# Pre-norming the next tile's input through a ring in unused FFN scratch, loading the residual copy afterwards, and new transfer constants for the scheduler

## The chip, the cores and the metric

One Trainium2 chip, all 8 cores of it (cores 0 to 3 are one die, 4 to 7 the other). Each core runs the same program on its own half of a sequence. The metric is the device time of the slowest core in microseconds. In the profiles PE is TensorE (matmuls), DVE VectorE, ACT ScalarE, POOL GpSimd and SP SyncE; L482 is line 482 of the kernel, and a bracket at the end of a line gives the idle time before it and what ended it.

A program on all 8 cores has two states here. In a *fast* execution the cores end close together (0.2 to 0.8% apart in most). In a *slow* one the cores of one die, sometimes of both, show a lower granted TensorE clock and end later, by 1.5 to 18% here. The value of a die is the median of its four spans; it counts as undisturbed if that lies within 0.3% of the lowest die of the same kernel's runs.

## The reference, cut to what matters

Four layers. Even ones mix tokens by a gated unit (mixer A), odd ones by causal pooling (mixer B). Each is followed by a SwiGLU FFN, and each half-layer has a norm before and after:

```python
for i in range(DEPTH):                        # DEPTH = 4
    h = rmsnorm(x, mix_pre_g[i])              # pre-norm
    m = mixer_a(h, ...) if i % 2 == 0 else mixer_b(h, ...)
    x = x + rmsnorm(m, mix_post_g[i])         # post-norm, residual
    h = rmsnorm(x, ffn_pre_g[i])
    f = swiglu(h, ...)
    x = x + rmsnorm(f, ffn_post_g[i])
```

x is (4, 8192, 1024) in float32. A core takes 4096 tokens and a halo of 256, in five tiles: a short first one (384 + 384 tokens) and four of 512 + 384. All four layers run on a tile before the next tile is loaded.

## The kernel before

The author writes tasks, a list scheduler simulates them with costs of its own, and the order it finds is what each engine executes. On the chip an engine goes through its list in order (in the changed kernel VectorE stood 6.11 us at one multiply whose load was late, and SQF, the next of its list, behind it); only the semaphore waits adjust to what really happens. The scheduler's picture of transfers is one server:

```python
    DMA_BW = 230e3          # bytes per us
    DMA_LAT = 2.2           # us
    # ... in place():
            if t.dma is not None:
                server[0] = max(server[0], now + 0.5) + t.dma / self.DMA_BW
                t.finish = server[0] + self.DMA_LAT
```

A pre-norm is: eight Squares on ScalarE into SQ, their running sum on VectorE (ACC, then SQF), one matmul with a matrix of ones that sums over partitions, Ln and Exp for 1/rms (RS), and eight multiplies on VectorE that write H, the operand of the next matmuls. After the last FFN of a tile the chain of a half (`v.h` is 0 for the 512 tokens, 1 for the 384) is:

```python
        def add(fc):
            # ... o is MS when this is the tile's last layer, X otherwise
            # o = MS * g + X                      (VectorE, line L605)
            if final is not None:
                y0, nx = final
                t_dma("sp", (0, s, v.h, fc), yT3[:, fc, y0:y0 + v.n], m, ...)   # store
                if nx is not None:
                    load_x(nx[0], v.h, nx[1], fc, s)       # next tile, into X, in place
            if st is not None:
                st.add(fm(X, nxt[0], fc), ...)             # Square and sum of the new X
        # ... mult and add for all eight fc, then
        if st is not None:
            st.rstd()
            prenorm_apply(nxt[0], s, nxt[1])               # H of the next tile
```

So the next tile's X can be loaded only when the last residual add has read the old one. Weights go through six slots of 1 MB (WR), filled by loads that GpSimd's queue issues and that convert float32 to bf16 on the way (1024 KB each in the trace); X, stores and constants are issued by SyncE's queue. BIG is a scratch of 32 chunks per half; an FFN uses 22 of them.

## Time and profile before

| | us |
|---|---|
| timed runs | 6520.97, 6594.38 (slow), 6279.75, later 6280.7 (fast) |
| profiled run (fast), eight cores | 6258.5 to 6284.9, granted clock 0.967 to 0.970 |
| PE idle in gaps over 0.15 us | 429 to 459, by core |
| PE idle between two tiles, core 3 | 29.5 at the first change, 38 to 40 at the other three |

The views that carry the argument are shown in the prediction. One more belongs here, because it says how the 40 us at a tile change come about: the DMA queues between 2323 and 2372 us, core 3 of the kernel before. The first two lines are packets, MB and the share of the 16 engines' time, the others the loads, KB each and median us from issue to landing.

```profile
q0 software_dynamic: 864, 6.29, 80.8%
q1 hardware_dynamic: 1336, 2.45, 16.2%
...
WR<-wa_in POOLq DMA_DIRECT2D x6, 1024.0 KB, 16.0
...
X<-xT SPq DMA_DIRECT2D x8, 256.0 KB, 32.7
```

Six weight loads that nobody needs yet (PE has no H to multiply them with) take five times as much of the DMA engines as the X loads and stores that everything waits for. A load of a quarter of the size lands after twice the time.

That the weights are what delays X at a tile change is read from this view and from the X loads' times; no run held the weights back there (run 8 does so at the program's start alone).

### The profile page before, as it was taken

How to read it: one execution, taken by the hardware profiler on the slowest of the kernel's cores; microseconds unless marked ns; L12 is line 12 of the kernel's file. 1: busy time of each engine (PE TensorE's matmuls, PEld its weight loads, DVE VectorE, ACT ScalarE, POOL GpSimd, SP SyncE). 2: the span in 40 equal slices, each digit the busy share in tenths (PEclk: the TensorE clock that was granted, in tenths of full speed). 3: DMA queues.
4: the chain of work that ended last, by engine and by line, in shares of the span. 5: the costliest groups of instructions: out<-in, count | busy, mean ns of one | idle time of the engine just before them, and what ended most of it. 6: DMA issues, size and time to landing. Idle time of an engine off the chain costs nothing.

```text
span 6284.9 us, 92435 instructions; the slowest of 8 cores (6258.5 to 6284.9 us)
## 1 busy us (share of the span) xinstructions
PE 5807.5 (92%) x33076; PEld 3088.8 (49%) x33076; DVE 2703.9 (43%) x4972; ACT 2505.9 (40%) x5135; POOL 257.3 (4%) x489
## 2 busy tenths in 40 slices
PE   5989887999999997999999969999999789999998
PEld 2655554444545543455544534554455345554554
DVE  3443533436353624443545245353634252635262
ACT  4343442525252515342534244245324342525252
POOL 0000000000000000000000000000000000000000
PEclk9999988999999998999999989999999899999999
DMA  6667778443554454444544445444444444454443
GB/s 134 116 108 115 132 132 151 79 85 75 96 96 78 79 98 101 87 87 82 96 88 84 78 91 101 98 82 88 82 95 81 107 89 74 85 97 81 74 89 76
DMA packets 117567, 592.36 MB, mean 94 GB/s; under 512 B 28032, under 2 KB 40704, under 8 KB 50944
## 3 DMA queue, kind: packets, MB, share of 16 engines
q0 software_dynamic: 69840, 507.82, 45.7%
q1 hardware_dynamic: 47280, 78.63, 3.8%
q8 instruction: 274, 4.49, 0.3%
q14 instruction: 173, 1.42, 0.1%
HBM read 1070.60 MB, written 23.59 MB: 174 GB/s over the span
## 4 chain that ended last, share of the span: by engine, by line
PE 77%; DVE 10%; issue 5%; DMA 4%; ACT 3%; SPq 0%; DVEq 0%; ACTq 0%
PE ps L482 77%; DVE ACC L546 3%; DMA X<-xT 3%; DVE MS L599 3%; DVE H L574 1%; ACT RS L463 1%; ACT SQ L463 1%; DVE MS L765 1%; DVE X L605 1%; ACT BIG L463 1%; DVE SQF L549 1%; DMA w_s<-BIG 1%; ACT L463 1%; SPq L492 0%; DVE BIG L735 0%
## 5 line engine op out<-in xcount | busy, mean ns | idle before, releaser
L482 PE MATMUL ps<-H,WR 128*128 128x384 bf16 (+3 forms) x16640 | 2980.7, 342 | 58.4 <-DVE H L574 45.3
L482 PEld LDWEIGHTS ps<-H,WR 128*128 128x128 bf16 x16640 | 1599.9, 98 | 1418.4 <-issue 104.5
L482 PE MATMUL ps<-BIG,WR 128*128 128x384 bf16 (+4 forms) x10880 | 1955.1, 340 | 14.8 <-ACT SQ L463 4.7
L482 PEld LDWEIGHTS ps<-BIG,WR 128*128 128x128 bf16 x10880 | 1041.5, 98 | 904.8 <-issue 45.7
L662 DVE TENSOR_TENSOR BIG<-ps,SG 128x384 bf16<-128x384 f32 (+5 forms) x880 | 515.7, 590 | 1554.7 <-PE ps L482 1424.6
L463 ACT ACTIVATE SG<-ps 128x384 bf16<-128x384 f32 (+5 forms) x880 | 448.7, 517 | 1597.4 <-PE ps L482 1590.9
L546 DVE TENSOR_TENSOR ACC<-ACC,SQ 128x384 f32<-128x384 f32 (+5 forms) x960 | 566.9, 593 | 857.9 <-ACT SQ L463 785.0
L482 PE MATMUL ps<-WR,H 128*128 128x512 bf16 x3216 | 736.0, 390 | 40.0 <-DVE H L574 38.1
L463 ACT ACTIVATE MS<-ps 128x384 f32<-128x384 f32 (+5 forms) x640 | 332.5, 520 | 1035.1 <-PE ps L482 1033.5
L463 ACT ACTIVATE BIG<-ps 128x512 bf16<-128x512 f32 (+2 forms) x914 | 479.7, 564 | 325.0 <-PE ps L482 282.3
L482 PEld LDWEIGHTS ps<-WR,H 128*128 128x128 bf16 x3216 | 319.3, 100 | 439.6 <-issue 89.0
L463 ACT ACTIVATE SQ<-X 128x384 bf16<-128x384 f32 (+4 forms) x640 | 343.2, 556 | 317.1 <-DMA X<-xT 136.2
L599 DVE TENSOR_TENSOR MS<-MS,RS 128x384 f32<-128x384 f32 (+5 forms) x640 | 367.6, 585 | 211.5 <-ACT RS L463 211.5
L463 ACT ACT_TABLE_LOAD x257 | 329.7, 1283 | 238.6 <-PE ps L482 205.3
L574 DVE SCALAR_TENSOR_TENSOR H<-X,GV,RS 128x384 bf16<-128x384 f32 (+4 forms) x640 | 371.1, 650 | 102.3 <-ACT RS L463 102.1
L605 DVE SCALAR_TENSOR_TENSOR X<-MS,GV,X 128x384 f32<-128x384 f32 (+5 forms) x560 | 356.0, 646 | 0.1
L463 ACT ACTIVATE SQ<-ps 128x384 bf16<-128x384 f32 (+5 forms) x640 | 329.5, 522 | 21.2 <-DVE ACC L546 12.6
L482 PE MATMUL ps<-SQF,ONESM 128*128 128x384 bf16 (+5 forms) x160 | 57.6, 360 | 279.0 <-DVE SQF L549 278.0
L765 DVE SCALAR_TENSOR_TENSOR MS<-ps,GV,BIAS 128x384 f32<-128x384 f32 (+2 forms) x320 | 197.1, 656 | 107.9 <-PE ps L482 107.7
L492 POOL DMA_DIRECT2D WR<-wf_gu x220 | 116.1, 528 | 2641.8 <-PE ps L482 2625.6
L544 DVE CAST ACC<-SQ 128x384 f32<-128x384 bf16 (+4 forms) x160 | 57.7, 372 | 309.6 <-ACT SQ L463 309.4
L463 ACT ACTIVATE RS<-ps,EPSC 128x384 f32<-128x384 f32 (+5 forms) x160 | 98.0, 613 | 215.4 <-PE ps L482 214.4
(45 smaller groups left out, 1234.6 us busy)
## 6 DMA issues: line engine op xcount, KB each, us to landing
WR<-wf_gu POOLq DMA_DIRECT2D x220, 1024.0 KB, 10.1
WR<-wf_dn POOLq DMA_DIRECT2D x120, 1024.0 KB, 8.6
WR<-wa_in POOLq DMA_DIRECT2D x80, 1024.0 KB, 11.3
WR<-wa_out POOLq DMA_DIRECT2D x40, 1024.0 KB, 10.5
WR<-wb_in POOLq DMA_DIRECT2D x20, 1024.0 KB, 10.2
WR<-w_s SPq DMA_DIRECT2D x20, 1024.0 KB, 7.4
X<-xT SPq DMA_DIRECT2D x48, 192.0 KB, 7.2
BIAS<-bias_s SPq DMA_DIRECT2D x9, 1024.0 KB, 7.9
```

The lines of the kernel that those rows point to most:

```text
L463: return e.activation(out=out() if callable(out) else out, in_=in_() if callable(in_) else in_, func=func, **kw)
L482: return e.matmul(out(), lhsT=lhsT() if callable(lhsT) else lhsT, rhs=rhs() if callable(rhs) else rhs, start=start, stop=stop)
L492: return e.dma_start(out=out() if callable(out) else out, in_=in_)
L544: t_dve(self.prio + (1,), lambda e: e.tensor_copy(out=acc, in_=o()), [kq], [ka], v.n, 2)
L546: t_dve(self.prio + (1,), lambda e: e.tensor_tensor(out=acc, in0=acc, in1=o(), op=ALU.add), [kq, ka], [ka], v.n)
L549: t_dve(self.prio + (1,), lambda e: e.tensor_tensor(out=fin, in0=acc, in1=o(), op=ALU.add), [kq, ka], [kfin], v.n)
L574: t_dve(CH + (s, v.h, 1), lambda e, o=o, a=a, g=g, r=r: e.scalar_tensor_tensor(out=o, in0=a, scalar=g, in1=r, op0=ALU.mult, op1=ALU.mult), ...
L599: t_dve(CH + (s, v.h, 0), lambda e: e.tensor_tensor(out=m, in0=m, in1=r, op=ALU.mult), kf("MS", v, fc) + [("RS", v.h)], kf("MS", v, fc), v.n)
L605: t_dve(CH + (s, v.h, 0), lambda e: e.scalar_tensor_tensor(out=o, in0=m, scalar=g, in1=x, op0=ALU.mult, op1=ALU.add), kf("MS", v, fc) + kf ...
L662: t_dve((0, s, v.h), lambda e, o=o, sg=sg, bu=bu: e.tensor_tensor(out=o, in0=bank(bu, 0, v.n), in1=sg(), op=ALU.mult), [bu, ksg], ko, v.n)
L765: t_dve((0, s, v.h), lambda e, b=b, o3=o3, bb=bb, lg=lg: e.scalar_tensor_tensor(out=o3, in0=bank(b, 0, nl * 128).rearrange("p (c t) -> p c ...
```

## The change

Intent: while the last FFN of a tile runs, chunks 22 to 31 of BIG are free. Stream the next tile's x through three float32 slots there, twice. The first pass makes the sum of squares and 1/rms, the second, as soon as the FFN head (its gate and up projections) no longer reads H, writes the next tile's H. X itself is loaded after the final add as before, but is now needed only by the residual add behind the next mixer. The scheduler's transfer constants are changed too, to two servers.

```diff
-    DMA_BW = 230e3
-    DMA_LAT = 2.2
+    DMA_BW = {"pool": 320e3, "sp": 150e3}
+    DMA_LAT = {"pool": 3.5, "sp": 5.0}
@@ place()
-                server[0] = max(server[0], now + 0.5) + t.dma / self.DMA_BW
-                t.finish = server[0] + self.DMA_LAT
+                server[e] = max(server[e], now + 0.5) + t.dma / self.DMA_BW[e]
+                t.finish = server[e] + self.DMA_LAT[e]
@@ class Stats: accumulator, final sum and result may lie in the ring; Squares keep their order (cut)
+    def prefetch(s, tok0, v, gcol):
+        h, n, hw = v.h, v.n, HW[v.h]
+        base = 22 * hw
+        # f32(lo, w): a float32 view of BIG from base + lo (cut)
+        def load(fc):
+            o, ko = f32((fc % 3) * 2 * hw, n)
+            t_dma("sp", (1, s, h, fc), o, xT3[:, fc, tok0:tok0 + n], [], ko, 128 * n * 4, psem[h][fc % 3])
+            return o, ko
+        st = Stats(v, (2, s, h), acc=..., fin=...)
+        held = {}
+        for fc in range(KC):
+            held[fc] = o, ko = load(fc)
+            st.add(o, ko, False)
+        st.rstd()
+        for i in range(KC):
+            fc = (i + KC - 3) % KC
+            a, ka = held[fc] if i < 3 else load(fc)
+            # H[fc] = a * g[fc] * r      (VectorE, line L621)
@@ chain()
-        st = Stats(nxt[0], CH + (s, v.h)) if nxt is not None else None
+        st = Stats(nxt[0], CH + (s, v.h)) if nxt is not None and final is None else None
-            if st is not None:
+            elif st is not None:
@@ the last FFN of a tile, between head and down projection
+            if s % 8 == 7 and t + 1 < NTILES:
+                for h in range(2):
+                    prefetch(s, tile_geo(t + 1)[h][0], nxt[h][0], nxt[h][1])
```

More of the change, by code (lines that the diff above doesn't have):

```diff
@@ L132, in place @@
         aset = [None]
-        server = [0.0]
+        server = {"pool": 0.0, "sp": 0.0}
         order = []
@@ L528, in build_nc, with __init__ @@
     class Stats:
-        def __init__(self, v, prio):
-            self.v, self.prio, self.i = v, prio, 0
+        def __init__(self, v, prio, acc=None, fin=None):
+            self.v, self.prio, self.i, self.last = v, prio, 0, None
+            self.acc, self.ka = acc or (ACC[v.h][:, v.c0:v.c1], [("ACC", v.h)])
+            self.fin, self.kfin = fin or (SQF[v.h][:, v.c0:v.c1], [("SQF", v.h)])
+            self.r, self.kr = acc or (RS[v.h][:, v.c0:v.c1], [("RS", v.h)])
         def add(self, src, ksrc, psum, aset=None):
@@ L536, in add @@
             kq, o = tmp(SQ, "SQ", v.n)
-            t_act(self.prio + (0,), o, src, AF.Square, ksrc, [kq], v.n, psum, alloc=kq)
+            t = t_act(self.prio + (0,), o, src, AF.Square, ksrc, [kq], v.n, psum, alloc=kq)
+            if self.last is not None:
+                t.preds.setdefault(self.last, -1.0)
+            self.last = t
             i = self.i
             self.i += 1
-            acc = ACC[v.h][:, v.c0:v.c1]
-            fin = SQF[v.h][:, v.c0:v.c1]
-            ka, kfin = ("ACC", v.h), ("SQF", v.h)
+            acc, fin, ka, kfin = self.acc, self.fin, self.ka, self.kfin
             if i == 0:
-                t_dve(self.prio + (1,), lambda e: e.tensor_copy(out=acc, in_=o()), [kq], [ka], v.n, 2)
+                t_dve(self.prio + (1,), lambda e: e.tensor_copy(out=acc, in_=o()), [kq], ka, v.n, 2)
             elif i < KC - 1:
                 t_dve(self.prio + (1,), lambda e: e.tensor_tensor(out=acc, in0=acc, in1=o(), op=ALU.add),
-                      [kq, ka], [ka], v.n)
+                      [kq] + ka, ka, v.n)
             else:
                 t_dve(self.prio + (1,), lambda e: e.tensor_tensor(out=fin, in0=acc, in1=o(), op=ALU.add),
-                      [kq, ka], [kfin], v.n)
+                      [kq] + ka, kfin, v.n)
         def rstd(self):
@@ L554, in rstd @@
             b = Var("pss")
-            fin = SQF[v.h][:, v.c0:v.c1]
-            r = RS[v.h][:, v.c0:v.c1]
+            fin, r, kr = self.fin, self.r, self.kr
             t_pe((-1,) + self.prio, [(lambda: bank(b, 0, v.n), ONESM[:], fin, True, True,
-                                      [("SQF", v.h), ("ONESM",)], [b], v.n)], alloc=b)
-            t_act(self.prio + (0,), r, lambda: bank(b, 0, v.n), AF.Ln, [b, ("EPSC",)], [("RS", v.h)], v.n,
+                                      self.kfin + [("ONESM",)], [b], v.n)], alloc=b)
+            t_act(self.prio + (0,), r, lambda: bank(b, 0, v.n), AF.Ln, [b, ("EPSC",)], kr, v.n,
                   bias=EPSC[:], aset="ln")
-            t_act(self.prio + (0,), r, r, AF.Exp, [("RS", v.h)], [("RS", v.h)], v.n, False, scale=-0.5, aset="ln")
+            t_act(self.prio + (0,), r, r, AF.Exp, kr, kr, v.n, False, scale=-0.5, aset="ln")
     CH = (1,)
@@ L590, in build_nc, with f32 @@
     yT3 = yT.rearrange("(fc p) t -> p fc t", p=128)
+    psem = [[newsem() for _ in range(3)] for _ in range(2)]
+    def prefetch(s, tok0, v, gcol):
+        h, n, hw = v.h, v.n, HW[v.h]
+        base = 22 * hw
+        def f32(lo, w):
+            return BIG[h][:, base + lo:base + lo + 2 * w].bitcast(F32), blocks(h, base + lo, 2 * w)
+        def load(fc):
+            o, ko = f32((fc % 3) * 2 * hw, n)
+            t_dma("sp", (1, s, h, fc), o, xT3[:, fc, tok0:tok0 + n], [], ko, 128 * n * 4, psem[h][fc % 3])
+            return o, ko
+        st = Stats(v, (2, s, h), acc=f32(6 * hw, n), fin=(BIG[h][:, base + 8 * hw:base + 8 * hw + n],
+                                                           blocks(h, base + 8 * hw, n)))
+        held = {}
[6 more added lines that the diff above has]
+            a, ka = held[fc] if i < 3 else load(fc)
+            o, g = fm(H, v, fc), GV[:, gcol + fc: gcol + fc + 1]
+            t_dve((2, s, h), lambda e, o=o, a=a, g=g: e.scalar_tensor_tensor(
+                out=o, in0=a, scalar=g, in1=st.r, op0=ALU.mult, op1=ALU.mult),
+                ka + st.kr + [("GV",)], kf("H", v, fc), n)
     def chain(v, s, gpost, nxt, final=None):
         r = RS[v.h][:, v.c0:v.c1]
-        st = Stats(nxt[0], CH + (s, v.h)) if nxt is not None else None
+        st = Stats(nxt[0], CH + (s, v.h)) if nxt is not None and final is None else None
         def mult(fc):
```

## The prediction

> **What bounds the kernel now.** I began with the spans of the eight cores (6258 to 6285 us, clock 0.967 to 0.970: the profiled execution is a fast one, although two of the three timed runs, 6520.97 and 6594.38 us, are not), then the page's busy line.
>
> ```profile
> PE 5807.5 (92%) x33076; PEld 3088.8 (49%) x33076; DVE 2703.9 (43%) x4972; ACT 2505.9 (40%) x5135; POOL 257.3 (4%) x489
> ```
>
> TensorE is the bound; what can be won is its idle time, 6284.9 - 5807.5 = 477 us, plus matmuls that run on a reduced clock. Next I took the list of waits (total, times, longest), to see who keeps PE and ScalarE idle.
>
> ```profile
> DVE ACC L546 <- ACT SQ L463: 785.0, 340, 13.9
> PE ps L482 <- DVE SQF L549: 278.0, 54, 49.1
> ACT SQ L463 <- DMA X<-xT: 136.2, 38, 13.9
> PE ps L482 <- DVE H L574: 83.4, 33, 6.0
> ```
>
> PE's largest wait is for the sum of squares (SQF) of a norm. SQF waits for Squares, Squares for the input load. To see where, I read PE's timeline at the change from the second tile to the third (start, duration, then in brackets the idle time before and its releaser).
>
> ```profile
> 2321.40 24.86 PE L482 MATMUL ps<-BIG,WR 128*128 128x384 bf16 x152
> 2364.03 0.48 PE L482 MATMUL ps<-SQF,ONESM 128*128 128x384 bf16 x1 [17.76 <-DVE SQF L549]
> 2383.13 0.58 PE L482 MATMUL ps<-SQF,ONESM 128*128 128x512 bf16 x1 [18.62 <-DVE SQF L549]
> 2386.33 29.51 PE L482 MATMUL ps<-WR,H 128*128 128x512 bf16 x128 [2.62 <-DVE H L574]
> ...
> 2445.65 0.48 PE L482 MATMUL ps<-SQF,ONESM 128*128 128x384 bf16 x1 [5.15 <-DVE SQF L549]
> 2449.57 23.41 PE L482 MATMUL ps<-WR,H 128*128 128x512 bf16 x96 [3.44 <-DVE H L574]
> ```
>
> The last down projection ends at 2346.26, and the new tile's first matmul starts at 2386.33: 17.76 + 18.62 + 2.62 = 39.0 us idle. The second token half follows only at 2449.57, after another 8.6 us in the last two lines. ScalarE's timeline there says why:
>
> ```profile
> 2345.84 0.63 ACT L463 ACTIVATE SQ<-X 128x512 bf16<-128x512 f32 x1 [8.42 <-DMA X<-xT]
> 2360.24 0.63 ACT L463 ACTIVATE SQ<-X 128x512 bf16<-128x512 f32 x1 [13.38 <-DMA X<-xT]
> 2371.84 0.63 ACT L463 ACTIVATE SQ<-X 128x512 bf16<-128x512 f32 x1 [6.04 <-DMA X<-xT]
> ```
>
> X is overwritten in place, so its load is issued only after the final residual add, at the moment when the freed weight slots start six 1 MB loads and the outputs are stored. The stretches show it (length, busy per engine, granted clock, DMA share, GB/s):
>
> ```profile
> 1841.00:1863.00 22.00, 22.00 (x113) 10.74 (x111) 4.15 (x6) 9.19 (x16) 0.00 (x0) 1.00 0.00 1
> 2288.00:2323.00 35.00, 35.00 (x172) 16.68 (x171) 4.93 (x8) 8.94 (x16) 0.00 (x0) 1.00 0.00 1
> 2346.00:2386.00 40.00, 1.33 (x4) 0.21 (x2) 15.89 (x30) 9.96 (x19) 0.53 (x1) 0.54 1.00 250
> ```
>
> In the last one the DMA engines are full (1.00) and PE is empty. In the first two, which are out-projections, the DMA engines are empty (0.00) and PE is full.
>
> [...] an X load took 3.7 us at best, 11.4 in the median and 47.4 at worst, the worst beside weights. [...] The trace has 257 loads of 1283 ns[...]: the load at 2321.65 took 1.28 and the next activation began at 2322.94.
>
> **The change part by part.** *Removed:* at each of the four tile changes, the wait of Squares, SQF and H for X. For its worth I don't add single gaps but compare whole stages. From the last down-projection matmul to the first matmul of the following FFN lies the same mixer-A work, inside a full tile and after a tile change. Inside a tile (layer 1 to 2), these are the ends of that stage (PE's timeline, and the chain that ended last):
>
> ```profile
> 1721.80 1.46 PE L482 MATMUL ps<-BIG,WR 128*128 128x384 bf16 x8
> ```
> ```profile
> 1884.40 178.89 PE ps L482 x915
> ```
>
> That is 1884.40 - 1723.26 = 161.1 us. After the tile change above it is 2565.69 - 2346.26 = 219.4, so 58.3 more: 39.0 of first gap, 8.6 of second, and about 11 of short waits in mixer A and matmuls at half clock. The other changes by the same reading: 1260.41 - 1066.46 = 194.0 (+32.8; it follows the short tile 0), 3873.23 - 3653.30 = 219.9 (+58.8), 5180.27 - 4960.43 = 219.8 (+58.7). Sum: 208.6 us. This is what a perfectly hidden pre-norm would win.
>
> *Moved:* 16 Squares, 16 accumulations, two Ln/Exp pairs and 16 H multiplies per change. The durations stay (Square 0.63 us for 512 columns, ACC 0.69, H 0.67). The placed order of the changed program puts the first pass (8 loads per half through three ring slots) beside mixer A's out-projection of layer 2, the first quiet stretch above; and the second pass (three slots still held, 5 loads, 8 multiplies per half) after the last FFN head has released H, the second quiet stretch. The loads there have the DMA engines to themselves. The H multiplies, 8 x 0.67 + 8 x about 0.54 = 9.7 us of VectorE, fit into a 66 us down projection in which it was busy 4.93 of 35.
>
> *Added:* 10 loads per change, (5 x 256 + 5 x 192 KB) x 4 = 9 MB on 592 MB: nothing. X itself is still loaded after the stores and landed by about 2386, but its next reader is the residual add behind mixer A's out-projection, over 150 us later.
>
> *Given back:* (a) In mixer A of layer 2 PE already waits for the first half's post-norm and next pre-norm (2.48 + 3.12 us before 1884.40). The order puts two ring accumulations (0.55 + 0.69) and a ring Square into that chain on VectorE and ScalarE, which run in program order: about 1.5 us, and 3 with one late landing. (b) The ring's Ln and Exp stand singly between Silus of the next FFN head; by the order's functions I count 24 more table loads, 6 per tile, 7.7 us of ScalarE. It was busy 20.5 of 51 us there and PE did not wait for it, so I give them 0 to 2. (c) The scheduler's transfer constants changed as well and reorder the short first tile: plus or minus 10, taken as +3. Sum 4 x 4 + 3 = 19.
>
> Total: 6285 - 209 + 19 = 6095 us in the fast state, 3.0% less.
>
> **Rivals.** (1) *The ring loads become the new wait.* There are 26 per change, and a load that lands late stops ScalarE or VectorE in order, in the midst of evacuations that PE needs. For it: X loads of 18.9 us in the median for 256 KB. Against: those were beside weights; in the out-projections a PSUM bank is filled in 16 or 22 matmuls, 3.4 to 4.7 us, and there are seven, so a stop of 10 us or more reaches nobody. If every tile lost 25 us: 6180. (2) *The tile change finds its next limit.* Output stores, X loads and six weight loads still collide at full DMA share. Mixer A's spatial step must wait until the stores have left MS, and a first weight must be there. Against: a first weight issued at 2323 needs some 10 us (the medians of such loads are 8.6 to 11.3), 13 us before its use; the stores were done by about 2386, while the spatial step comes some 61 us after the down projection, about 2407. If I am wrong by 15 us in three changes: 6140. (3) *Only half is won*, because H is released late and the second half's multiplies are not ready: the gap of 8.6 us and the stutter after it would stay: 6155. (4) The load was hidden anyway: excluded by the three ScalarE lines.
>
> **Range and chances.** Fast runs: 6060 (all of the 209, and a wait less in the new order) to 6180 (rival 1). But the time of the kernel before was put down as 6520.97, a slow run, 3.8% above its fastest (6279.75); the other slow one was 5.0% above. If the median of the changed kernel is a slow run too, 6095 becomes about 6330 to 6400. I can't tell the state beforehand, so the range is 6060 to 6400 and the value is that of the fast state. For 2% the kernel must come to 6159 or less: 126 of the 209 us have to stay. That falls only if rival 1 is strong or two rivals come together: faster 0.87, within 2% 0.12, slower 0.01.
>
> **What would show it.** Right: no SQF wait over 5 us at the four tile changes in PE's timeline; down-projection end to next FFN 158 to 168 us; ScalarE's wait for X gone but for the start; ring loads landing in 4 to 8 us; PE idle of about 280 us instead of 454 (the sum of its gaps over 0.15 us); table loads about 280. Wrong: waits of Squares on the ring's loads with PE waits behind them in layer 2's mixer A; a wait for MS or WR after the tile change; PE's waits at layer 2's FFN grown from 5.6 to over 15 us.

## The result, and the profile after

| | kernel before | changed kernel |
|---|---|---|
| fast runs | 6279.75, 6280.7 | 6062.69, 6067.45 |
| slow runs | 6520.97, 6594.38 | 6326.12, 6828.85, 6420.38, 6414.75 |
| PE idle, gaps over 0.15 us, core 5 | 429 | 248 |
| granted clock, fast | 0.967 to 0.970 | 0.984 to 0.986 |

The ratio of the fast runs is 0.9657 (95% interval 0.9616 to 0.9699): 3.4% faster. Ratios in this document are the mean time of one kernel's fast runs over that of the other's of the same rounds, so not quite the ratio of the medians quoted.

The profiled run of the changed kernel is slow on cores 0 to 3. I read core 5, of the undisturbed die (span 6052.9, clock 0.985), against core 5 of before (6262.3). First its waits, to be held against the four lines of the prediction (L554 is what L549 was, L621 the H multiply from the ring):

```profile
PE ps L482 <- DVE SQF L554: 113.2, 42, 43.2
...
PE ps L482 <- DVE H L578: 59.2, 25, 4.5
...
ACT SQ L463 <- DMA X<-xT: 24.3, 4, 7.0
...
DVE H L621 <- DMA BIG<-xT: 19.4, 12, 6.1
ACT SQ L463 <- DMA BIG<-xT: 18.0, 7, 5.5
```

PE's wait for SQF fell from 260.4 (core 5 of before; 278.0 on core 3) to 113.2, and 43.2 of what is left is the start of the program. ScalarE's wait of Squares for X fell from 34 times (38 on core 3) to 4, all at the start. Two new small waits on the ring's loads stand at the end. PE's timeline at the same tile change as in the prediction:

```profile
2264.55 22.26 PE L482 MATMUL ps<-BIG,WR 128*128 128x384 bf16 x136
2286.65 0.59 PE L482 MATMUL ps<-WR,H 128*128 128x512 bf16 x2
2287.08 1.46 PE L482 MATMUL ps<-BIG,WR 128*128 128x384 bf16 x8
...
2290.11 2.32 PE L482 MATMUL ps<-WR,H 128*128 128x512 bf16 x10
2292.27 0.33 PE L482 MATMUL ps<-SQF,ONESM 128*128 128x384 bf16 x1
2292.43 45.49 PE L482 MATMUL ps<-WR,H 128*128 128x512 bf16 x210
```

The new tile's matmuls (WR,H) start before the last down projection (BIG,WR) has ended, and no line has a bracket. The 40 us after it, in the columns of the prediction's third window, which they match:

```profile
2290.00:2330.00 40.00, 40.00 (x188) 18.15 (x187) 8.63 (x17) 32.55 (x95) 2.11 (x4) 1.00 1.01 188
```

The DMA engines are as full as before (1.01). The collision of weights, stores and X loads is still there; but nobody waits for it, and PE is busy 40.00 of 40.00. The loads of the changed kernel (KB each, median us to landing):

```profile
BIG<-xT SPq DMA_DIRECT2D x52, 256.0 KB, 5.5
BIG<-xT SPq DMA_DIRECT2D x52, 192.0 KB, 7.8
...
X<-xT SPq DMA_DIRECT2D x32, 256.0 KB, 37.1
```

The same 256 KB takes 5.5 us where the prefetch puts it and 37.1 where the residual copy is loaded. The change has not made the transfer faster where it was; it has moved the urgent one to a quiet place and left a patient one in the queue.

To find where the time went I cut PE's timeline at two marks per tile, the end of the last down projection and the first matmul of the FFN after mixer A, and call what lies between "the change". Core 5, us:

| | before | after | gain |
|---|---|---|---|
| start to the end of tile 0 | 1062.5 | 1043.1 | 19.4 |
| change 1 (after the short tile) | 189.0 | 159.1 | 29.9 |
| rest of tile 1 | 1085.8 | 1088.1 | -2.3 |
| change 2 | 217.0 | 159.5 | 57.5 |
| rest of tile 2 | 1086.9 | 1090.1 | -3.2 |
| change 3 | 215.8 | 159.1 | 56.7 |
| rest of tile 3 | 1087.6 | 1089.8 | -2.2 |
| change 4 | 213.5 | 159.1 | 54.4 |
| rest | 1104.4 | 1105.0 | -0.6 |
| sum | 6262.3 | 6052.9 | 209.4 |

(The parts are rounded and add to 209.6.) Of the 209.4 us, 180.7 are gaps of PE (429.2 before, 248.5 after), and most of the rest is PE's busy time, 5809.9 before and 5781.5 after: core 5 spent 393.2 us of the span at half clock before and 184.6 after, and its mean clock in changes 2 to 4 rose from between 0.86 and 0.88 to over 0.99. In the prediction's third window, where PE was busy for 1.33 of 40 us, the clock was 0.54, and in the 14 us of matmuls after it 0.86 (core 3 of before). The changes give 198.5 us, about as forecast. Tile 0 gives 19.4 that were not forecast, and there PE's timeline has a wait that the other changes don't have. First PE, then VectorE shortly before it:

```profile
992.91 19.09 PE L482 MATMUL ps<-BIG,WR 128*128 128x128 bf16 x232
1020.20 0.27 PE L482 MATMUL ps<-SQF,ONESM 128*128 128x128 bf16 x1 [8.20 <-DVE SQF L554]
```
```profile
1006.78 0.75 DVE L621 SCALAR_TENSOR_TENSOR H<-BIG,GV 128x512 bf16<-128x512 f32 x1 [4.86 <-DMA BIG<-xT]
...
1018.57 1.28 DVE L621 SCALAR_TENSOR_TENSOR H<-BIG,GV 128x512 bf16<-128x512 f32 x2 [6.11 <-DMA BIG<-xT]
1019.77 0.28 DVE L554 TENSOR_TENSOR SQF<-ACC,SQ 128x128 bf16<-128x128 f32 x1
```

VectorE stands at an H multiply whose load is late by 6.11 us (it was issued beside weight loads and took 10 us), and SQF, which comes next in its list, stands behind it; PE then stands at SQF. This is the prediction's first rival, in one place. So two questions were left for experiments: what tile 0's 19.4 us are made of, and which parts of the change carry the rest.

### The profile page after: what moved, and what is told of

The parts are those of the page before. It is cut to its first block, busy times and chain, and to the rows that moved or that the text cites. A ratio compares the mean times of both kernels' runs of the same rounds, so it can differ in the third digit from the quotient of the medians.

```text
span 6324.6 us, 92294 instructions; the slowest of 8 cores (6050.6 to 6324.6 us)
## 1 busy us (share of the span) xinstructions
PE 6022.3 (95%) x32685; PEld 3161.4 (50%) x33076; DVE 2703.4 (43%) x4972; ACT 2526.3 (40%) x5147; POOL 257.3 (4%) x489
## 4 chain that ended last, share of the span: by engine, by line
PE 83%; DVE 7%; issue 4%; DMA 3%; ACT 3%; DVEq 0%; SPq 0%; ACTq 0%
PE ps L482 83%; DVE ACC L551 2%; DVE MS L632 2%; DMA BIG<-xT 1%; DVE H L578 1%; ACT RS L463 1%; DMA X<-xT 1%; ACT SQ L463 1%; ACT BIG L463 1%; DMA w_s<-BIG 1%; DVE X L638 1%; ACT L463 0%; DVE SQF L554 0%; DVE MS L798 0%; DMA MS<-wb_grpT 0%
## 5 line engine op out<-in xcount | busy, mean ns | idle before, releaser
L482 PE MATMUL ps<-H,WR 128*128 128x384 bf16 (+5 forms) x16468 | 3109.5, 352 | 97.2 <-DVE H L578 71.9
L482 PEld LDWEIGHTS ps<-H,WR 128*128 128x128 bf16 x16640 | 1639.3, 101 | 1519.3 <-issue 370.3
L482 PE MATMUL ps<-BIG,WR 128*128 128x384 bf16 (+5 forms) x10776 | 2050.8, 352 | 25.5 <-DVE MS L798 5.0
L551 DVE TENSOR_TENSOR ACC<-ACC,SQ 128x512 f32<-128x512 f32 (+5 forms) x912 | 537.1, 591 | 776.0 <-ACT SQ L463 705.3
L463 ACT ACTIVATE BIG<-ps 128x512 bf16<-128x512 f32 (+1 forms) x914 | 480.6, 563 | 369.7 <-PE ps L482 333.7
L463 ACT ACT_TABLE_LOAD x269 | 345.1, 1283 | 177.8 <-PE ps L482 112.8
L463 ACT ACTIVATE SQ<-X 128x384 bf16<-128x384 f32 (+4 forms) x576 | 304.1, 552 | 167.8 <-DVE ACC L549 54.7
L578 DVE SCALAR_TENSOR_TENSOR H<-X,GV,RS 128x384 bf16<-128x384 f32 (+4 forms) x576 | 332.0, 646 | 85.6 <-ACT RS L463 85.1
L463 ACT ACTIVATE SQ<-BIG 128x512 bf16<-128x512 bf16 (+2 forms) x332 | 203.4, 625 | 34.3 <-DMA BIG<-xT 24.9
L803 DVE TENSOR_TENSOR BIG<-MS,BIG 128x384 bf16<-128x384 f32 (+3 forms) x320 | 174.2, 583 | 0.0
L463 ACT ACTIVATE RS<-ps,EPSC 128x512 f32<-128x512 f32 (+5 forms) x152 | 92.8, 610 | 201.9 <-PE ps L482 201.2
```

The source lines that it names most:

```text
L463: return e.activation(out=out() if callable(out) else out, in_=in_() if callable(in_) else in_, func=func, **kw)
L482: return e.matmul(out(), lhsT=lhsT() if callable(lhsT) else lhsT, rhs=rhs() if callable(rhs) else rhs, start=start, stop=stop)
L551: t_dve(self.prio + (1,), lambda e: e.tensor_tensor(out=acc, in0=acc, in1=o(), op=ALU.add), [kq] + ka, ka, v.n)
L578: t_dve(CH + (s, v.h, 1), lambda e, o=o, a=a, g=g, r=r: e.scalar_tensor_tensor(out=o, in0=a, scalar=g, in1=r, op0=ALU.mult, op1=ALU.mult), ...
L803: t_dve((0, s, v.h), lambda e, u=u, tv=tv: e.tensor_tensor(out=u, in0=tv, in1=u, op=ALU.mult), kf("MS", v, fc % 8) + ku, ku, v.n)
```

## The experiments

All ran correct, each beside the kernel before on the same chip. "Undisturbed" is the median of the undisturbed dies (as many as in brackets); the kernel before has 6271.5, 6266.5 and 6269.7 in the three calls, the changed kernel 6054.0 (8) in its first runs. "Changes 2 to 4" are stages as in the table above, on one core of an undisturbed die of the profiled run. Where a row has 159 the cores of the run agree within a microsecond, but the longer stages differ by core: in the kernel before by up to 6 us (change 4: 213.5 to 219.9), in runs 4 and 5 by up to 9, and change 1 of the ring of two by 11. The end of tile 0 differs by up to 20 us between cores of one run. So each row names its core, and where tile 0 matters below I compare several.

| run (core) | undisturbed | tile 0 ends | change 1 | changes 2 to 4 |
|---|---|---|---|---|
| before (5) | about 6269 | 1062.5 | 189.0 | 217.0, 215.8, 213.5 |
| changed (5) | 6054.0 (8) | 1043.1 | 159.1 | 159.5, 159.1, 159.1 |
| changed, again (1) | 6060.9 (5) | 1045.8 | 159.1 | 159.5, 159.1, 159.1 |
| constants alone (5) | 6206.7 (7) | 1021.7 | 198.5 | 204.5, 204.4, 203.4 |
| changed, old constants (1) | 6096.8 (3) | 1070.7 | 181.7 | 159.5, 159.1, 159.3 |
| statistics alone (5) | 6173.2 (4) | 1045.1 | 170.7 | 191.2, 191.7, 190.9 |
| first half alone (1) | 6152.4 (8) | 1031.1 | 184.2 | 188.9, 187.0, 187.4 |
| ring of two (1) | 6053.9 (6) | 1042.6 | 170.5 | 159.8, 159.1, 159.1 |
| later ring in tile 0 (1) | 6038.6 (7) | 1026.4 | 159.1 | 159.4, 159.1, 159.1 |
| X before weights (1) | 6029.1 (4) | 1023.3 | 159.1 | 159.5, 159.1, 159.1 |
| both (1) | 6014.6 (8) | 1004.6 | 159.1 | 159.4, 159.1, 159.2 |

**1. The changed kernel again.** No edit.

> The changed kernel again, unaltered, for a fast profile of all cores and as the measure for the other runs of this call. Expected: fast runs 6050 to 6070 us, ratio to the kernel before 0.964 to 0.968; on a fast core PE idle (gaps over 0.15 us) about 250 us, 8 us of it one wait for SQF at the first tile change.

All six runs were slow on one die or both, so there is no fast run and no ratio. The undisturbed dies gave 6058.8 to 6063.2, cores 6052 to 6069. On core 1 PE idled 6.9 to 7.2 us in each change, on core 0 8.2 to 8.6. It repeats.

**2. The constants alone**, on the kernel before:

```diff
-    DMA_BW = 230e3
-    DMA_LAT = 2.2
+    DMA_BW = {"pool": 320e3, "sp": 150e3}
+    DMA_LAT = {"pool": 3.5, "sp": 5.0}
     # and server[0] -> server[e], as in the change
```

> The kernel before with the scheduler's new transfer constants and nothing else (no ring, no prefetch). Theory A (my reading of the two traces: some 30 us of the gain come from a better order of the short first tile, which the constants alone produce): about 6250 us, ratio 0.995, with the first tile's end some 30 us earlier and the four waits at the tile changes as long as before (30 to 40 us each on PE). Theory B (the constants matter only together with the ring; the prediction put 3 us of loss on them): 6275 to 6290 us, ratio 0.999 to 1.002.

Better than both theories: undisturbed 6206.7, 65 us less (the verdict on fast runs, 0.9934, interval 0.9838 to 1.003, rests on two runs of which one has a die 40 us behind; it can't tell). Tile 0 ended 40.8 us earlier on core 5, not 30. And the changes, which I had expected unaltered, moved too: change 1 became 9.5 us longer, changes 2 to 4 each 10 to 12.5 us shorter. PE's timeline at one of the latter, core 5:

```profile
2332.37 0.48 PE L482 MATMUL ps<-SQF,ONESM 128*128 128x384 bf16 x1 [25.80 <-DVE SQF L549]
2344.77 0.58 PE L482 MATMUL ps<-SQF,ONESM 128*128 128x512 bf16 x1 [11.92 <-DVE SQF L549]
2348.18 21.71 PE L482 MATMUL ps<-WR,H 128*128 128x512 bf16 x88 [2.82 <-DVE H L574]
2369.73 0.33 PE L482 MATMUL ps<-SQF,ONESM 128*128 128x384 bf16 x1
```

The first gap is no shorter: 25.80 + 11.92 + 2.82 = 40.5 us, against 36.4 at the same change on core 5 of before and 39.0 on core 3. The second, of the other half (5.15 + 3.44 us in the prediction's lines), is gone: the norm of that half now stands inside the first half's matmuls (last line) and not behind mixer A's. So the forecast's 58 us per change held two things: some 45 that stay as long as X is waited for, and some 12 that a better order alone takes away.

For tile 0, PE's order of instructions in this run and in the changed kernel is the same up to the first ring instruction at 690 us (the kernel before parts from it within the first mixer), and the ring has no part in it: the constants made that part. Most of it is won early: the first FFN starts at 183.7 us here and at 182.6 in the changed kernel, against 214.4 before (all core 5). Which of the four, and by which turn of the scheduler, stays open.

**3. The change with the old constants**, the edit of run 2 reversed on the changed kernel.

> The changed kernel with the scheduler's old transfer constants (one server, 230 GB/s, 2.2 us). Theory A (prefetch and constants add up): 6090 to 6100 us, ratio 0.970 to 0.972, tile changes still free of waits, the first tile 30 us longer. Rival: the old constants make the scheduler believe in loads that land early, so VectorE and ScalarE stop in order at ring loads in all four tile changes: PE waits of 5 to 20 us per change come back, 6120 to 6170 us, ratio 0.975 to 0.983.

6096.8: theory A (the one fast run, 6124.96, has a die 20 us behind the other). Changes 2 to 4 are as short as with the new constants. "Add up" is too much, though: the constants alone won 65 us and the ring alone 175 (6271.5 - 6096.8), 240 together, but both in one kernel won 211 (run 1). Once the ring is there, the constants win nothing at a full change; they win in tile 0 (1070.7 against 1045.8, both core 1) and change 1 (181.7 against 159.1). The rival, stops at ring loads in all tiles, is out; in change 1, which I had expected free of waits, it holds: PE waits 6.83 us for an SQF, which stands behind a ring multiply on VectorE that waited 6.17 for its load, and 6.10 for an H multiply from the ring.

**4. Statistics alone**: the ring's first pass as in the change, but H is made from X.

```diff
-        for i in range(KC):                  # second pass through the ring
-            ...
+        pre[h] = st
@@ chain(), after the final add and load_x
+        for fc in range(KC):                 # H = X * g * r, r from the ring
+            t_dve(CH + (s, v.h, 1), ..., kf("X", n, fc) + p.kr, kf("H", n, fc), n.n)
```

> Only the first pass is prefetched (sum of squares and 1/rms from the ring); H is made from X after X's load behind the final add, as before. Theory A (the wait is for X's landing, which queues behind weights and stores; the statistics are a small part): the PE gap at the tile changes stays at 25 us or more each, 6170 to 6220 us, ratio 0.983 to 0.990. Rival (the chain of Squares, SQF, Ln and Exp is most of the wait): the gap falls below 12 us, 6080 to 6120 us, ratio 0.969 to 0.975.

Theory A: 6173.2 and a fast run of 6192.28, stage 191. PE's gaps are now single ones between the first matmuls of the tile; VectorE, then PE:

```profile
2319.91 0.75 DVE L654 SCALAR_TENSOR_TENSOR H<-X,GV,BIG 128x512 bf16<-128x512 f32 x1 [12.87 <-DMA X<-xT]
```
```profile
2320.80 1.87 PE L482 MATMUL ps<-WR,H 128*128 128x512 bf16 x4 [12.60 <-DVE H L654]
```

Each piece of H waits for its piece of X, and PE for H. Read against run 2, which has the same constants: of the 45 us per change (204 to 159) having the statistics early is worth about 13, having x itself early about 32 (core 5; other cores of this run lie up to 5 us beside it).

**5. The first half alone**:

```diff
-                for h in range(2):
-                    prefetch(s, tile_geo(t + 1)[h][0], nxt[h][0], nxt[h][1])
+                prefetch(s, tile_geo(t + 1)[0][0], nxt[0][0], nxt[0][1])
@@ chain()
+        old = final is None or v.h == 1
-        st = Stats(...) if nxt is not None and final is None else None
+        st = Stats(...) if nxt is not None and old else None
-            elif st is not None:
+            if st is not None:
```

> The changed kernel with the prefetch for the first token half alone; the second half's pre-norm runs from X after the final add, as before. Theory A (PE needs the second half as soon as the six weight slots hold no piece that the first half alone can use, some 40 us after the down projection, while X's second half lands after 60 to 70 us): a PE gap of 15 to 35 us per full tile change remains, stage from down projection to the next FFN 178 to 195 us (all: 159; none: 204), undisturbed cores 6110 to 6160 us. Rival (the first half's work covers the second half's wait): stage 160 to 166 us, undisturbed cores 6055 to 6080 us.

6152.4, ratio 0.9809 (0.9762 to 0.9857, so whether it reaches 2% is unclear), stage 187 to 189: theory A in the numbers. The way is partly another than I wrote, though. ScalarE's line at a change:

```profile
2334.15 0.52 ACT L463 ACTIVATE SQ<-X 128x384 bf16<-128x384 f32 x1 [14.20 <-DMA X<-xT]
```

PE did not only run out of work for the first half. ScalarE, in order, stood 14.20 us at a Square of the second half's X, and the first half's Gelus, which PE needed to go on, stood behind it (a PE wait of 5.13 us for them). Against run 2, about 16 of the 45 us per change were won (204.1 to 187.8 in the mean of three, core 5 against core 1; cores 2 and 3 of this run have 185.4 and 189.2), with half of the prefetch.

**6. A ring of two slots**: `fc % 3` becomes `fc % 2`, two slots held, six loads in the second pass.

> The ring cut from three slots to two: fewer loads in flight, 6 instead of 5 loads in the second pass. Theory A (in the full tiles the second pass has some 40 us of slack before the next tile's first matmul): stage after a full tile change stays at 159 to 162 us, undisturbed cores 6053 to 6080 us, any loss sits in the short first tile. Rival (the ring is already at its limit): PE waits for H at the tile changes, 5 to 15 us each, undisturbed cores 6085 to 6130 us.

6053.9, ratio 0.9666 (0.9593 to 0.974): no difference to three slots. Changes 2 to 4 are unaltered. Change 1 is 11 us longer on core 1, 5 to 7 on cores 2, 3 and 7, and no longer on cores 4 and 5; core 1's span is 9 longer than in run 1 (6063.8 against 6054.8), but the medians of the dies show no difference (6053.9 against 6054.0 and 6060.9). At a full change the ring is not at a limit.

**7. Later ring in tile 0**: the scheduler is told that the ring's loads of the short first tile land 10 us later than its constants say. Nothing else moves.

```diff
-                t.finish = server[e] + self.DMA_LAT[e]
+                t.finish = server[e] + self.DMA_LAT[e] + t.lag
@@ prefetch(), load()
+            t.lag = 10.0 if s < 8 else 0.0
```

> The scheduler is told to expect the ring's loads of the short first tile 10 us later (no other load, no other tile), so that Squares, accumulations and H multiplies stand later in the engines' order. Theory A (the 16 to 20 us that the first tile costs with the ring against without it come from engines that stop in program order at late ring loads; among them the 8 us wait of PE for SQF at the first change): these shrink by half or more, undisturbed cores 6040 to 6052 us. Rival (the cost is the added work or the other order of matmuls, not the late landings): 6053 to 6070 us as in the changed kernel, or longer.

6038.6 and a fast run of 6044.64: theory A. The end of tile 0, core by core (the constants alone and the changed kernel's first run have the other die undisturbed, so only pairs of lines are of the same cores):

| | core | core | core | core |
|---|---|---|---|---|
| constants alone, cores 4 to 7 | 1033.5 | 1021.7 | 1030.8 | 1024.2 |
| changed, cores 4 to 7 | 1047.8 | 1043.1 | 1041.4 | 1040.8 |
| changed again, cores 0 to 3 | 1055.6 | 1045.8 | 1047.7 | 1055.4 |
| later ring, cores 0 to 3 | 1031.0 | 1026.4 | 1030.2 | 1035.9 |

The ring had cost tile 0 between 11 and 21 us by core (first pair); the later landing brings 17 to 25 back (second pair), which is about where the constants alone had it. The waits on ring loads (on the same core in run 1: 17.7 and 29.1) and PE's SQF at change 1, which has no bracket now, on core 1:

```profile
ACT SQ L464 <- DMA BIG<-xT: 4.8, 5, 1.8
...
DVE H L623 <- DMA BIG<-xT: 3.5, 5, 1.1
```
```profile
1005.84 0.22 PE L483 MATMUL ps<-SQF,ONESM 128*128 128x128 bf16 x1
```

Loads and work are the same; only the places in the lists differ. The loads did not get faster either: between 600 and 1030 us their medians to landing are 7.6 and 13.6 us (256 and 192 KB), against 4.4 and 10.4 on core 1 in run 1. So the cost of the ring in tile 0 was engines stopping in order at loads believed to be earlier.

**8. X before the weights, at the program's start.** Not a part of the change, but the same conflict where there is no earlier tile to hide it in:

```diff
+            if seq[0] == 0:
+                reads = [("X", 0, KC - 1)]      # the first weight load waits for the first half of X
             t = t_dma(eng, (0, seq[0]), ..., src, list(reads), [var], ...)
```

> The changed kernel, with the first weight load issued only when the first half of the first tile's X has landed (it was issued beside X, and X landed over 55 us). Not a part of the change, but the same mechanism at the only tile change without a tile before it. Theory A (X stands behind six weight loads): first matmul of mixer A at 25 to 35 us instead of 58, the weights then follow the matmuls closely, undisturbed cores 6020 to 6045 us. Rival (the weights, 8 us each, are the bound of the start in either order): no gain within 8 us.

6029.1; one run counted as fast, 6067.43, with a die 30 us behind the other. PE's start in the changed kernel (core 5) and in this run (core 0, of its undisturbed die):

```profile
54.54 0.48 PE L482 MATMUL ps<-SQF,ONESM 128*128 128x384 bf16 x1 [43.24 <-DVE SQF L554]
57.62 11.09 PE L482 MATMUL ps<-WR,H 128*128 128x512 bf16 x40 [2.60 <-DVE H L578]
```
```profile
26.02 0.48 PE L482 MATMUL ps<-SQF,ONESM 128*128 128x384 bf16 x1 [13.14 <-DVE SQF L556]
31.63 4.18 PE L482 MATMUL ps<-WR,H 128*128 128x512 bf16 x10 [5.13 <-DMA WR<-wa_in]
```

The first matmul comes at 31.63 and not at 57.62, and PE is then held by its first weight for 5.13 us. Theory A.

**9. Both** edits of 7 and 8.

> Both edits of the first tile together on the changed kernel: the ring's loads of the first tile expected 10 us later by the scheduler, and the first weight load behind the first half of X. Theory A (they mend two separate waits, one at the start and one in the second half of the first tile, so they add): undisturbed cores 6005 to 6018 us (about 6058 minus 20 minus 29), start of the first FFN near 158 us, first tile's last down projection ended near 1000 us; ratio to the kernel before about 0.958. Rival (both recover the same slack): 6025 to 6040 us, as the better of the two alone.

6014.6 (eight dies), one fast run of 6022.53 beside fast runs of before of 6279.88 to 6313.75. That is 24 below run 7 and 14.5 below run 8, in the expected 6005 to 6018. The two nearly add up: alone they win 19 and 28 against the mean of 6054.0 and 6060.9, which makes 47; together they win 43. This is the version that beats both kernels: its undisturbed dies are at 6014.6 / 6269.7 = 0.959 of the kernel before, against 0.966 of the changed one.

## Why the prediction was right or wrong

*The bound, and the worth of the wait: right.* The forecast's 208.6 us were read on core 3; the same reading on core 5, whose stages were shorter, gives 190.5 (the four stages less 4 x 161.2). Core 5 won 198.5 in the four changes. The stages came out at 159.1 to 159.5, in the forecast's 158 to 168, even a little below the 161.2 inside a tile, because the norm of the second half no longer lies there. That stage difference held, as run 2 shows, more than the wait for X (45 of 57). I had put all of it on X, and that the sum did not suffer is luck in part: run 3 shows that the ring takes away all 57 with the old constants too. PE's idle time fell by 180.7 us on core 5, with 174 forecast (454 to 280, core 3).

*Moved and added work: right.* The loads landed in 5.5 and 7.8 us in the median (forecast 4 to 8). The quiet place was not quite as quiet as I had it, though: the first loads of the first pass stood beside a weight load and took 8 us, and those of the second pass beside the last one of the down projection. The residual copy of X landed 72 us after the down projection (2362 against 2290), not 40 as I had said, because PE does not stop now and frees weight slots during that time: the loads of wa_in and wa_out issued between 2302 and 2350 stand beside it. That is a reading of the trace; no run takes them away. Its reader came later still.

*Given back, (a) and (b): right in kind, somewhat too high.* Forecast 4 us per tile; tiles 1 to 3 lost 2.3, 3.2 and 2.2. The chain of (a) took 0.8 to 1.2 of it, not 1.5 to 3: mixer A inside these tiles went from 161.2 to between 162.0 and 162.4 us on core 5, and PE's two waits at its end from 5.6 to 6.8 at most. Of table loads there are 12 more, not 24:

```profile
L463 ACT ACT_TABLE_LOAD x269 | 345.1, 1283 | 164.5 <-PE ps L482 131.9 <-DMA X<-xT 23.0 <-DVE ST L761 6.2
```

Before there were 257; my count from the order was double the truth. Each took 1283 ns, and the next activation began within 0.02 us of a load's end.

*Given back, (c): this step failed.* "The scheduler's transfer constants changed as well and reorder the short first tile: plus or minus 10, taken as +3." With 4 us of (a) and (b) in tile 0 I had 7 us of loss there; core 5 gained 19.4. These 26 us are most of the miss of 30 between 6095 and the mean of 6062.69 and 6067.45. (The terms don't add up exactly, since the forecast was read on core 3: on core 5 the changes gave 10 less than 208.6, and tiles 1 to 3 lost 4 less than forecast.) Two large terms stood in it: the constants alone won 40.8 us (run 2), and the ring cost 21.4 of them again (1043.1 against 1021.7, core 5; 11 to 21 by core), which a later assumed landing gives back (run 7). I had seen that the order of tile 0 changed and had set a small number on it without reading how much idle time the old order had there.

*The rivals.* (1), ring loads as a new wait: refuted for the full tiles (runs 1 and 3), true in the first one, 8.2 us in a single wait and 11 to 21 in all, by core. (2), the next limit behind the old one: no such wait appeared, although the DMA engines stayed full. (3), only half is won: not so; run 5 shows what it would have looked like, and that in-order ScalarE carries it. (4): excluded, as said.

*The range.* The fast runs lie in 6060 to 6400, at its lower end. The median of the first four runs, 6417.57, all of them slow, lies above it: the forecast for a slow median, 6330 to 6400, was too narrow. Slow runs of the changed kernel took 6190 to 7120, and those of before up to 7367, while I had two to judge from.

## What to carry to other kernels

When an input that is overwritten in place starts every tile, look for scratch that is idle in the stage before, and move only what the next matmul needs into it; the rest of the transfer may stay where it collides, if its reader is far off (here X took 37.1 us to land, and only the program's start waited for it). What such a wait is worth is best read by comparing a whole stage with and without it, and a changed scheduler constant deserves its own run, because it can be worth as much as a part of the change (65 of 209 us alone, here). Work that fills gaps on an in-order engine is only as harmless as its loads are punctual (one stop of 6.11 us on VectorE made PE wait 8.20 us): tell the scheduler a late landing rather than a likely one where other transfers run.
